# Two mixture layers of a transformer block: put-back behind the next up product, another routing sequence

## The chip, the cores and the metric

The kernel runs on one core of a Trainium2 chip. The core has TensorE (matrix products; PE in the rows), VectorE (DVE), ScalarE (ACT), GpSimd (POOL) and SyncE (SP), which here only issues DMAs, and DMA engines that bring the weights from memory. Each engine works through its own instructions in order and waits on semaphores for the others. The metric is the device time of one execution in microseconds.

## The reference

A block of two layers with mixtures of experts is followed by a second block of four layers without them. Only the mixtures are touched. Each takes 256 tokens of 1024 features, 16 experts in four groups of four, and two experts a token:

```python
scores = sigmoid(hf @ router_w)                      # 256 x 16
sel = (scores + router_bias).reshape(n, 4, 4)
group_score = top_k(sel, 2)[0].sum(-1)
g = argmax(group_score)                              # one group a token
in_group = take_along_axis(sel, g_idx, axis=1)[:, 0]
_, local = top_k(in_group, 2)                        # two experts in it
w = take_along_axis(scores, idx) ; w = w / w.sum()
combine = sum(one_hot(idx, 16) * w[..., None], axis=1)
for e in range(16):
    a = silu(hf @ w_gate[e]) * (hf @ w_up[e])        # 1024 -> 512
    y = y + combine[:, e:e+1] * (a @ w_down[e])      # 512 -> 1024
```

`hf` is the normalised and modulated input; the result, times a gate, is added to the residual stream `x`.

## The kernel before

Layer 0 of the mixtures runs from about 204 to 481 us of the profiled execution, layer 1 from about 655 to 923 us. `_moe` (L1289) does one layer.

Routing (`route`, L1172): TensorE transposes `x` into `xT` (L1181), ScalarE copies it out (L1183); 16 products give the logits with `xT` as the stationary side (L1188); VectorE scales them (`lg`), ScalarE takes the sigmoid (`sc`), and VectorE ranks experts in their groups and then the groups (`ranks`, L1214: greater, equal, three adds, a sum) down to the 0/1 choice `top` (L1234) and the weights `comb` (L1241). Meanwhile `x` times the inverse norm is kept as a rounded high part `hh` (ScalarE, L1202) and a low part `hl` (ScalarE L1206 and GpSimd L1207). Both are shown as `hTh` and `hTl` in the rows. Prefix sums of `top` on TensorE (L1303 to L1307) give each token its place `pos` (L1313) among the 64 slots of its expert.

`gather(g)` (L1327) serves four experts: a one-hot matrix `oh` (VectorE, L1335) is multiplied with high and low parts (32 products, four PSUM banks, L1344), the banks are scaled into `xgt`, masks `back` for the way home are made (L1357, L1359), and the combine weights `cs` in slot order (L1366).

Then experts follow one another. `up(e+1)` (L1396) is 16 products in two halves of eight (L1405; gate and up side by side in column tiles of 64, so two run as a pair), then ScalarE copies them out. `act(e)` (L1412) is four transposes (L1418), silu on ScalarE and a product `sg` on VectorE. `down(e)` (L1424) is eight products (L1430); behind it VectorE scales (`dg`, L1435), ScalarE takes the high part `dv` (L1436) and VectorE the low part (L1437). `put_back(e)` (L1440) adds both parts to the four accumulators with eight products (L1447).

Weights, 6 MiB an expert, come through SyncE's queue in 1 MiB transfers. `fetch` takes the places in turn from a string `HOMES`: "r" a buffer of the common ring of five, "h" a pair of half-size buffers (six pairs), "x" a buffer of a ring of its own (`WX`, two). `MF` names the experts behind which loads for the next modulation are put into the same queue.

The order on each engine isn't the order of the code: a list scheduler of the framework picks, for each engine, the next instruction from its own costs. `issue_after(i)` keeps what is written in its scope behind instruction `i` in that order.

Of the kernel before, what the change touches and what calls it, by code (L numbers as in the profile page):

```python
# [20 lines left out]
S = 256  # L21
# [9 lines left out]
GU = 2  # L31
# [3 lines left out]
WX = 2  # L35
HOMES = "rhrhxhrhrhxhr"
# [47 lines left out]
class Net:  # L84
# [636 lines left out]
    def prepare(self):  # L721
# [32 lines left out]
        nc.vector.memset(self.ones, 1.0)  # L754

# [416 lines left out]
    def route(self, outer, r, hh, hl, rwA, rb, rsh, AS):  # L1172
# [4 lines left out]
        for tok in range(NT):  # L1177
            for half in range(2):
                ps = self.pacc()
                for k in range(4):  # L1180
                    nc.tensor.transpose(ps[:, k * 128:k * 128 + 128],  # L1181
                                        x[:, tok, half * 512 + k * 128:half * 512 + k * 128 + 128], self.ident)
                nc.scalar.copy(xT[:, half * 4:half * 4 + 4, tok * 128:tok * 128 + 128],  # L1183
                               ps.rearrange("p (k t) -> p k t", k=4))
# [28 lines left out]
        def ranks(v, n, name):  # L1213

            gt, eq, rk = t(name + "g", n, 4, 4), t(name + "e", n, 4, 4), t(name + "r", n, 4)
# [3 lines left out]
            nc.vector.tensor_tensor(eq, ot, me, OP.is_equal)  # L1219
            for i in range(4):  # L1220
                if i:
                    nc.vector.tensor_tensor(gt[:, :, i, 0:i], gt[:, :, i, 0:i], eq[:, :, i, 0:i], OP.add)
# [12 lines left out]
                                       top, op0=OP.is_lt, op1=OP.mult)  # L1235
        nc.vector.tensor_tensor(ts, top, sc, OP.mult)
# [6 lines left out]
        return top, comb  # L1243

    def router(self, layer, A, SH):
# [7 lines left out]
        rwA = self.b1.tile([128, 8, 16], F32, name="rwA", tag="rwA")  # L1253
        nc.vector.tensor_tensor(rwA, rw, A[:, :, None].to_broadcast([128, 8, 16]), OP.mult)
# [34 lines left out]
    def _moe(self, layer, G, router, hh, hl):  # L1289
# [7 lines left out]
        top, comb_ = self.route(outer, r, hh, hl, *router)  # L1297
# [7 lines left out]
        nc.tensor.matmul(ps[:, 16:32], self.ones, top[:, 0, :], start=False, stop=True)  # L1305
        for tok in range(NT):
            nc.tensor.matmul(ps[0:1, 32:48], self.ones[:, 0:1], top[:, tok, :], start=tok == 0, stop=tok == 1)  # L1307
        comb = outer.tile([128, NT, 16], F32, name="combk", tag="combk", bufs=1)
# [3 lines left out]
        pos = outer.tile([128, NT, 16], F32, name="pos", tag="pos", bufs=1)  # L1312
        nc.vector.scalar_tensor_tensor(pos, ps[:, 0:32].rearrange("p (t e) -> p t e", t=NT), 1.0, top, op0=OP.add,  # L1313
                                       op1=OP.mult)
# [12 lines left out]
        def gather(g, bank=self.pat):  # L1327


            oh = self.wk.tile([128, NT, 4, CAP], F32R, name="oh", tag="oh", bufs=1)  # L1330
# [4 lines left out]
            i = nc.vector.tensor_tensor(oh, self.slot[:, None, None, :].to_broadcast([128, NT, 4, CAP]),  # L1335
                                        pos[:, :, 4 * g:4 * g + 4, None].to_broadcast([128, NT, 4, CAP]), OP.is_equal)
            yield i
            for d0 in range(0, 8, 2):
                ps = bank()
                pds = [ps[:, d * 256:d * 256 + 256] for d in range(2)]  # L1340
                for d, pd in enumerate(pds, d0):
                    for s, src in enumerate((hh, hl)):
                        for tok in range(NT):
                            mm(pd, src[:, tok, d * 128:d * 128 + 128], oh[:, tok].rearrange("p e s -> p (e s)"),  # L1344
                               start=s == 0 and tok == 0, stop=s == 1 and tok == 1)
# [50 lines left out]
        def up(e, res):  # L1396
# [4 lines left out]
            for m in range(2):  # L1401
                ws = [fetch(near(w[e], 4 * m, 4), 4, 512) for w in (wg, wu)]
                for k in range(4):
                    for j in range(2):
                        mm(ps[j * CAP:j * CAP + CAP, :], xg[:, 4 * m + k, e % 4, :], ws[j][k],  # L1405
                           start=m == 0 and k == 0, stop=m == 1 and k == 3)
# [7 lines left out]
        def act(gu):  # L1414
# [4 lines left out]
            sg = self.wk.tile([128, 4, CAP], F32, name="sg", tag="sg")  # L1419
# [4 lines left out]
        def down(e, sg):  # L1424
# [9 lines left out]
            t = self.wk.tile([128, 512], F32, name="dg", tag="dg", bufs=1)  # L1434
# [16 lines left out]
        steps = gather(0, self.pacc)  # L1451
        last = next(steps)
        with self.tc.issue_after(last.ins):
            for _ in steps:
                pass
            cur = []
            for _ in up(0, cur):
                pass
# [3 lines left out]
        for e in range(16):  # L1462
# [8 lines left out]
            if dv is not None:  # L1471
                put_back(e - 1, dv)
# [180 lines left out]
```

## Time and profile before

| | us |
|---|---|
| median of three runs | 2383.67 (2382.63 to 2385.36) |
| profiled execution | 2383.23 |
| its span in the trace | 2381.4 |
| TensorE busy | 2255.3 (95%) |
| VectorE busy | 1285.7 (54%) |
| ScalarE busy | 986.2 (41%) |
| GpSimd busy | 10.3 |

The span runs from the first to the last instruction; the 1.8 us beyond it lie around the program. Busy shares are means over stages of different kinds; the two mixture layers, some 545 us of the 2381, are read by windows of their own below. In a row of the timeline stand the start, the length, the engine and line, what is written and read, and in brackets how long the engine had been idle and for whom. Matmuls overlap their neighbours a little, so steps are measured from start to start.

### The profile page before, as it was taken

How to read it: one execution, taken by the hardware profiler on the slowest of the kernel's cores; microseconds unless marked ns; L12 is line 12 of the kernel's file. 1: busy time of each engine (PE TensorE's matmuls, PEld its weight loads, DVE VectorE, ACT ScalarE, POOL GpSimd, SP SyncE). 2: the span in 40 equal slices, each digit the busy share in tenths (PEclk: the TensorE clock that was granted, in tenths of full speed). 3: DMA queues.
4: the chain of work that ended last, by engine and by line, in shares of the span. 5: the costliest groups of instructions: out<-in, count | busy, mean ns of one | idle time of the engine just before them, and what ended most of it. 6: DMA issues, size and time to landing. Idle time of an engine off the chain costs nothing.

```text
span 2381.4 us, 34230 instructions
## 1 busy us (share of the span) xinstructions
PE 2255.3 (95%) x13802; PEld 1763.2 (74%) x13802; DVE 1285.7 (54%) x2518; ACT 986.2 (41%) x1620; POOL 10.3 (0%) x12
## 2 busy tenths in 40 slices
PE   6998999979989997999999998999999999999998
PEld 3897433268954334888899897988988898887987
DVE  4885121288632115565655666555886556666554
ACT  3544111156431113443544564444664444434443
POOL 0000000000000000000000000000000000000000
PEclk9998999979889998999999999999999999999999
DMA  8877999967679995445566534555544565454552
GB/s 309 291 264 286 404 390 409 341 213 255 243 298 415 415 408 189 166 142 176 175 212 204 190 95 136 193 168 181 174 138 159 168 204 187 145 177 142 186 169 88
DMA packets 250056, 541.99 MB, mean 228 GB/s; under 512 B 15752, under 2 KB 158720, under 8 KB 236576
## 3 DMA queue, kind: packets, MB, share of 16 engines
q1 hardware_dynamic: 239936, 531.99, 63.0%
q10 hardware_dynamic: 9952, 7.70, 1.1%
q8 instruction: 113, 1.85, 0.3%
q14 instruction: 55, 0.45, 0.1%
HBM read 538.57 MB, written 4.22 MB: 228 GB/s over the span
## 4 chain that ended last, share of the span: by engine, by line
PE 53%; DVE 5%; ACT 1%; issue 1%; DMA 1%; ACTq 0%; SPq 0%; DVEq 0%
DVE wl L157 2%; ACT wh L156 1%; DVE rsa L263 0%; DVE rsy L267 0%; PE acc__mlp__13096 L201 0%; PE acc__mlp__19954 L201 0%; PE acc__mlp__9809 L201 0%; PE acc__mlp__13097 L201 0%; PE acc__mlp__16544 L202 0%; PE acc__mlp__19955 L201 0%; PE acc__mlp__16544 L201 0%; PE acc__mlp__9810 L203 0%; PE acc__mlp__13096 L202 0%; PE acc__mlp__19955 L203 0%; PE acc__mlp__9810 L201 0%
## 5 line engine op out<-in xcount | busy, mean ns | idle before, releaser
L157 DVE TENSOR_TENSOR wl<-raw,wh 128x1024 fp32r<-128x1024 f32 (+4 forms) x526 | 614.7, 1188 | 379.4 <-ACT wh L156 375.8
L156 ACT CAST wh<-raw 128x1024 fp32r<-128x1024 f32 (+4 forms) x526 | 524.6, 1023 | 477.0 <-issue 60.2
L833 DVE SCALAR_TENSOR_TENSOR macc<-raw,c,macc 128x1024 f32<-128x1024 f32 x84 | 107.4, 1278 | 0.4
L402 ACT CAST aTh<-rl 128x512 fp32r<-128x512 f32 x56 | 34.8, 621 | 78.5 <-DVE rl L400 78.5
L539 ACT ACTIVATE p<-p,m 128x128 f32<-128x128 f32 (+1 forms) x128 | 57.1, 448 | 19.7 <-DVE m L537 19.6
L1436 ACT CAST dv<-dg 128x512 fp32r<-128x512 f32 x32 | 19.8, 618 | 102.4 <-DVE dg L1435 102.4
L280 ACT ACTIVATE junk<-x 128x512 f32<-128x512 f32 x52 | 32.8, 631 | 66.5 <-DVE x L345 36.3
L403 DVE TENSOR_TENSOR aTl<-rl,aTh 128x512 fp32r<-128x512 f32 x56 | 38.8, 692 | 38.5 <-ACT aTh L402 38.5
L400 DVE TENSOR_TENSOR rl<-rl 128x512 f32<-128x512 f32 x56 | 38.4, 685 | 0.0
L263 DVE SCALAR_TENSOR_TENSOR rsa<-rsy,rsh 128x1 f32<-128x1 f32 x186 | 34.5, 217 | 2.6
L1437 DVE TENSOR_TENSOR dv<-dg,dv 128x512 fp32r<-128x512 f32 x32 | 22.1, 691 | 18.3 <-ACT dv L1436 18.3
L222 ACT CAST hTh<-xg 128x512 fp32r<-128x512 f32 (+1 forms) x36 | 21.1, 606 | 14.4 <-DVE xg L219 14.3
L1447 PEld LDWEIGHTS acc__moe__2303<-dv,back 64*128 64x128 f32 x32 | 5.7, 186 | 25.8 <-ACT dv L1436 16.3
L267 DVE SCALAR_TENSOR_TENSOR rsy<-rsa,rsy 128x2 f32<-128x2 f32 (+2 forms) x141 | 22.7, 161 | 3.2
L539 ACT ACTIVATION_READ_ACCUMULATOR p<-p,m 128x1 f32 x128 | 24.3, 190 | 0.0
L1447 PE MATMUL acc__moe__2303<-dv,back 64*128 64x512 f32 x32 | 15.2, 494 | 9.3 <-ACT dv L1436 8.3
L223 DVE TENSOR_TENSOR hTl<-xg,hTh 128x512 fp32r<-128x512 f32 (+1 forms) x36 | 23.4, 672 | 0.3
L1447 PEld LDWEIGHTS acc__moe__6191<-dv,back 64*128 64x128 f32 x32 | 5.4, 183 | 24.1 <-ACT dv L1436 14.3
L1447 PE MATMUL acc__moe__6191<-dv,back 64*128 64x512 f32 x32 | 14.3, 477 | 7.0 <-ACT dv L1436 6.5
L1447 PE MATMUL acc__moe__2304<-dv,back 64*128 64x512 f32 x32 | 15.4, 497 | 0.0
L502 DVE TENSOR_SCALAR oss<-oss 128x1 f32<-128x1 f32 x16 | 2.5, 154 | 22.2 <-ACT junk L501 22.2
L1447 PE MATMUL acc__moe__6192<-dv,back 64*128 64x512 f32 x32 | 14.3, 477 | 0.0
(3879 smaller groups left out, 7278.5 us busy)
## 6 DMA issues: line engine op xcount, KB each, us to landing
raw<-in_w_up_dram SPq DMA_DIRECT2D x64, 1024.0 KB
raw<-in_w_down_dram SPq DMA_DIRECT2D x64, 1024.0 KB
raw<-in_w_mod_dram SPq DMA_DIRECT2D x48, 1024.0 KB
raw<-in_ret_w_in_dram SPq DMA_DIRECT2D x48, 1024.0 KB
raw<-in_exp_w_gate_dram SPq DMA_DIRECT2D x40, 1024.0 KB
raw<-in_exp_w_down_dram SPq DMA_DIRECT2D x34, 1024.0 KB
raw<-in_exp_w_up_dram SPq DMA_DIRECT2D x30, 1024.0 KB
wh<-in_exp_w_up_dram SPq DMA_DIRECT2D x34, 512.0 KB
```

What stands on the lines that cost most here:

```text
L156: nc.scalar.copy(h[:, :m * n], p)
L157: eng.tensor_tensor(l[:, :m * n], p, h[:, :m * n].bitcast(F32), OP.subtract)
L223: nc.vector.tensor_tensor(lo[:, k0:k0 + n, tok * 128:tok * 128 + 128], pv, d.bitcast(F32), OP.subtract)
L263: nc.vector.scalar_tensor_tensor(a[:, c], y[:, c], h[:, c], y[:, c], op0=OP.mult, op1=OP.mult)
L267: nc.vector.scalar_tensor_tensor(y, a, 1.5, y, op0=OP.add, op1=OP.mult)
L280: self.sq = nc.scalar.activation(junk[:, :w], p, AF.Square, scale=n ** -0.5, accum_out=ss[:, i, j:j + 1]).ins
L400: nc.vector.tensor_tensor(rl, rl, rl, OP.mult)
L402: nc.scalar.copy(h, rl)
L403: nc.vector.tensor_tensor(aT[1][:, 2 * j:2 * j + 2, :].rearrange("p k t -> p (k t)"), rl, h.bitcast(F32), OP.subtract)
L539: nc.scalar.activation(p[:, m, :], p[:, m, :], AF.Exp, bias=mx[:, m:m + 1], accum_out=rs[:, m, s:s + 1])
L833: i = nc.vector.scalar_tensor_tensor(acc, r[:, k, :], self.c[:, kk:kk + 1], acc, op0=OP.mult, op1=OP.add)
L1447: mm(acc[tok][half], back[c, e % 4, tok * 128:tok * 128 + 128], dv[j][c, :], start=e == 0 and j == 0, stop=e == 15 and j == 1)
```

## The change

- `put_back(e - 1)` is issued behind the last matmul of the first half of the next up product (`half_up`).
- Buffers: the ring `x` has three places (`WX`), with a new string `HOMES` of 14 places; `gu` takes turns between two pools; `sg` uses the tiles `hm` of the modulation, `dg` two tiles of another pool; `oh` sits in the outer pool.
- Logits: `rwA`, padded to 32 columns, is now the stationary side, and four column tiles each sum two of the eight parts; a copy and two products with `four` (four identities under one another) add them up. One of the four copies of `xT` goes to VectorE.
- `ranks` has three comparisons and a sum: ties are handled by "greater or equal" in the lower triangle.
- `pos` and the first `oh` come ahead of `comb`, `most` and the others; the low parts are made by VectorE behind that `oh`, from `x`, the norm and `hh` in one operation each; GpSimd and the copies `xn` on ScalarE are gone.
- The first gather begins with the high parts of four of its eight slices; then the first up product follows before its masks and combine weights.

The core of the diff:

```diff
-WX = 2
-HOMES = "rhrhxhrhrhxhr"
+WX = 3
+HOMES = "rhxhrhrxhrhrxh"
...
+        pl = self.pat()
+        for k in range(8):
+            j = 32 * (k % 4)
+            nc.tensor.matmul(pl[j:j + 32, 0:S], rwA[:, k, :], xT[:, k, :], start=k < 4, stop=k >= 4)
+        lT = self.cm.tile([128, 512], F32, name="xg", tag="xg")[:, 0:S]
+        nc.scalar.copy(lT, pl[:, 0:S])
         pr = self.pat()
         for tok in range(NT):
-            for k in range(8):
-                nc.tensor.matmul(pr[:, tok * 16:tok * 16 + 16], xT[:, k, tok * 128:tok * 128 + 128], rwA[:, k, :],
-                                 start=k == 0, stop=k == 7)
+            nc.tensor.matmul(pr[:, tok * 16:tok * 16 + 16], lT[:, tok * 128:tok * 128 + 128], self.four, start=True,
+                             stop=True)
...
-                for half in range(2):
-                    c = slice(half * 512, half * 512 + 512)
-                    xn = self.cm.tile([128, 512], F32, name="xg", tag="xg")
-                    nc.scalar.mul(xn.rearrange("p (k q) -> p k q", k=4), xv[:, half], r[:, tok:tok + 1])
-                    nc.gpsimd.tensor_tensor(hl[:, tok, c], xn, hh[:, tok, c].bitcast(F32), OP.subtract)
...
             nc.vector.tensor_tensor(gt, ot, me, OP.is_gt)
-            nc.vector.tensor_tensor(eq, ot, me, OP.is_equal)
-            for i in range(4):
-                if i:
-                    nc.vector.tensor_tensor(gt[:, :, i, 0:i], gt[:, :, i, 0:i], eq[:, :, i, 0:i], OP.add)
+            nc.vector.tensor_tensor(gt[:, :, 2:4, 0:2], ot[:, :, 2:4, 0:2], me[:, :, 2:4, 0:2], OP.is_ge)
+
+            two = gt.rearrange("p n i j -> p n (i j)")[:, :, 4:15:10]
+            nc.vector.tensor_tensor(two, v[:, :, 0:3:2], v[:, :, 1:4:2], OP.is_ge)
...
+        first_oh, i = one_hot(0)
+        with self.tc.issue_after(i.ins):
+            for m in range(2):
+                c = slice(m * 512, m * 512 + 512)
+                for tok in range(NT):
+                    nc.vector.scalar_tensor_tensor(
+                        hl[:, tok, c].rearrange("p (k q) -> p k q", k=4), x[:, tok, c].rearrange("p (q k) -> p k q", k=4),
+                        r[:, tok:tok + 1], hh[:, tok, c].rearrange("p (k q) -> p k q", k=4).bitcast(F32), op0=OP.mult,
+                        op1=OP.subtract)
...
+            if early:
+                pss = [bank() for _ in range(4)]
+                for d in range(0, 8, 2):
+                    part(pss[d // 2][:, 0:256], d, 0)
...
                 if m == 0:
+                    self.half_up = i.ins
                     yield
-            t = self.wk.tile([128, 512], F32, name="gu", tag="gu", bufs=GU)
+            pool, tag = (self.jk, "junk") if e % 2 else (self.wk, "gu")
+            t = pool.tile([128, 512], F32, name="gu", tag=tag, bufs=1)
...
-            sg = self.wk.tile([128, 4, CAP], F32, name="sg", tag="sg")
+            sg = self.mods.tile([128, S], F32, name="hm", tag="hm", bufs=HM).rearrange("p (f c) -> p f c", c=CAP)
...
-            t = self.wk.tile([128, 512], F32, name="dg", tag="dg", bufs=1)
+            t = self.cm.tile([128, 512], F32, name="xg", tag="xg")
...
             if dv is not None:
-                put_back(e - 1, dv)
+                with self.tc.issue_after(self.half_up):
+                    put_back(e - 1, dv)
```

What this does to the order of the instructions is shown at three places. Tile names end in numbers that differ between the two programs; line numbers shift too (before and after: up L1405 and L1438, transposes L1418 and L1453, down L1430 and L1465, put-back L1447 and L1482, gather L1344 and L1365).

TensorE, layer 1, around the start of the up product of expert 13 (`pj`), with the down product of expert 12 (`at` from `sg` or `hm`). Before:

```order
L1430 MATMUL at__moe__7216<-wh,sg 64x512 x2
L1430 MATMUL at__moe__7216<-wl,sg 64x512 x2
L1418 MATMUL at__moe__7252<-ident,gu 128x128 x4
L1430 MATMUL at__moe__7216<-raw,sg 64x512 x4
L1405 MATMUL pj__moe__7237<-wh,xgt 64x512
L1447 MATMUL acc__moe__6191<-dv,back 128x512
L1447 MATMUL acc__moe__6192<-dv,back 128x512
L1447 MATMUL acc__moe__6193<-dv,back 128x512
L1447 MATMUL acc__moe__6194<-dv,back 128x512
```

Now:

```order
L1465 MATMUL at__moe__7179<-wh,hm 64x512 x2
L1453 MATMUL at__moe__7213<-ident,gu 128x128 x4
L1465 MATMUL at__moe__7179<-wl,hm 64x512 x2
L1438 MATMUL pj__moe__7200<-raw,xgt 64x512 x8
L1438 MATMUL pj__moe__7200<-wh,xgt 64x512
L1482 MATMUL acc__moe__6158<-dv,back 128x512
L1482 MATMUL acc__moe__6159<-dv,back 128x512
```

Six more rows of put-back follow here, and then the last seven of the up product. The put-back has moved from behind the first up matmul to behind the ninth.

TensorE, layer 0, from the logits to the start of the gather. Before:

```order
L1188 MATMUL at__moe__2107<-rwA,xT 128x16 x16
L1303 MATMUL at__moe__2177<-top,first 128x16
L1304 MATMUL at__moe__2177<-top,first 128x16
L1305 MATMUL at__moe__2177<-top,ones 128x16
L1307 MATMUL at__moe__2177<-top,ones 1x16 x2
L1319 MATMUL at__moe__2191<-ident,pos 16x128 x2
L1344 MATMUL acc__moe__2202<-oh,hTh 128x256 x2
L1344 MATMUL acc__moe__2202<-oh,hTl 128x256 x2
```

Now:

```order
L1192 MATMUL at__moe__2113<-xT,rwA 32x256 x8
L1197 MATMUL at__moe__2124<-four,xg 128x16 x2
L1310 MATMUL at__moe__2156<-top,first 128x16
L1311 MATMUL at__moe__2156<-top,first 128x16
L1312 MATMUL at__moe__2156<-top,ones 128x16
L1333 MATMUL at__moe__2156<-top,ones 1x16 x2
L1343 MATMUL at__moe__2182<-ident,pos 16x128 x2
L1365 MATMUL acc__moe__2191<-oh,hTh 128x256 x2
L1365 MATMUL acc__moe__2192<-oh,hTh 128x256 x2
L1365 MATMUL acc__moe__2193<-oh,hTh 128x256 x2
L1365 MATMUL acc__moe__2194<-oh,hTh 128x256 x2
L1365 MATMUL acc__moe__2191<-oh,hTl 128x256
```

The logits are eight products and two small ones instead of 16, and the high parts of four slices stand ahead of the first low part.

VectorE, layer 0, from `top` to the one-hot. Before:

```order
L1234 SCALAR_TENSOR_TENSOR top<-grr,top 128x32
L1236 TENSOR_TENSOR ts<-top,sc 128x32
L1238 TENSOR_REDUCE tot<-ts 128x2
L1239 RECIPROCAL tot<-tot 128x2
L1311 TENSOR_REDUCE most<-at__moe__2177 1x1
L1241 TENSOR_TENSOR comb<-ts,tot 128x32
L1313 SCALAR_TENSOR_TENSOR pos<-at__moe__2177,top 128x32
L1309 COPY combk<-comb 128x32
L1316 SCALAR_TENSOR_TENSOR over<-pos,combk 128x32
L1335 TENSOR_TENSOR oh<-first,pos 128x512
```

Now:

```order
L1238 SCALAR_TENSOR_TENSOR top<-grr,top 128x32
L1241 TENSOR_TENSOR ts<-top,sc 128x32
L1243 TENSOR_REDUCE tot<-ts 128x2
L1314 SCALAR_TENSOR_TENSOR pos<-at__moe__2156,top 128x32
L1244 RECIPROCAL tot<-tot 128x2
L1319 TENSOR_TENSOR oh<-first,pos 128x512
L1328 SCALAR_TENSOR_TENSOR hTl<-x,rsy,hTh 128x512 x4
L1246 TENSOR_TENSOR comb<-ts,tot 128x32
L1338 TENSOR_REDUCE most<-at__moe__2156 1x1
L1336 COPY combk<-comb 128x32
L1345 CAST posT<-at__moe__2182 16x256
L1340 SCALAR_TENSOR_TENSOR over<-pos,combk 128x32
```

`pos` and `oh` have moved ahead of `comb`, `most`, `combk` and `over`, and the four low parts have come in behind `oh`.

## Rows read from the trace of the kernel before

**Rows 1.** The page: busy time of the engines, shares of the chain.

```profile
PE 2255.3 (95%) x13802; PEld 1763.2 (74%) x13802; DVE 1285.7 (54%) x2518; ACT 986.2 (41%) x1620; POOL 10.3 (0%) x12
...
PE 53%; DVE 5%; ACT 1%; issue 1%; DMA 1%; ACTq 0%; SPq 0%; DVEq 0%
```

**Rows 2.** Windows: length, busy us of PE, PEld, DVE, ACT, POOL, clock, DMA share, GB/s.

```profile
225.69:293.62 67.93, 67.93 (x399) 31.48 (x399) 13.31 (x26) 9.31 (x18) 0.00 (x0) 1.00 0.93 365
293.62:480.59 186.97, 174.82 (x834) 63.82 (x830) 40.48 (x62) 23.12 (x44) 0.00 (x0) 0.99 0.95 374
676.30:770.21 93.91, 93.91 (x526) 41.38 (x526) 18.45 (x33) 14.19 (x27) 0.00 (x0) 1.00 0.96 382
770.21:922.98 152.77, 142.96 (x690) 51.66 (x687) 26.49 (x45) 18.41 (x35) 0.00 (x0) 0.99 0.91 364
```

**Rows 3.** Waits of TensorE, 204 to 490 us (total us, times, longest).

```profile
PE acc__moe__2303 L1447 <- ACT dv L1436: 8.3, 8, 1.6
...
PE at__moe__2957 L1366 <- DVE sg L1421: 0.9, 1, 0.9
```

**Rows 4.** The same, 655 to 930 us.

```profile
PE acc__moe__6191 L1447 <- ACT dv L1436: 6.5, 7, 1.6
```

**Rows 5.** TensorE timeline, a step of layer 1, 742 to 756 us (start, length).

```profile
742.38 0.59 PE L1405 MATMUL pj__moe__6547<-raw,xgt 128*64 128x512 f32 x1
...
745.92 0.66 PE L1418 MATMUL at__moe__6562<-ident,gu 128*128 128x128 f32 x4
746.50 0.64 PE L1405 MATMUL pj__moe__6547<-raw,xgt 128*64 128x512 f32 x1
...
750.09 0.49 PE L1447 MATMUL acc__moe__6191<-dv,back 64*128 64x512 f32 x1
...
751.21 0.50 PE L1344 MATMUL at__moe__6599<-oh,hTh 128*128 128x256 f32 x2
...
752.34 1.94 PE L1430 MATMUL at__moe__6610<-raw,sg 128*64 128x512 f32 x8
...
755.83 0.59 PE L1405 MATMUL pj__moe__6631<-raw,xgt 128*64 128x512 f32 x1
```

**Rows 6.** TensorE timeline, a late step, 868 to 885 us.

```profile
868.18 1.02 PE L1405 MATMUL pj__moe__7237<-wh,xgt 128*64 128x512 f32 x2
...
884.11 0.50 PE L1447 MATMUL acc__moe__6191<-dv,back 64*128 64x512 f32 x1 [1.56 <-ACT dv L1436]
...
884.77 1.07 PE L1405 MATMUL pj__moe__7305<-raw,xgt 128*64 128x512 f32 x2
```

**Rows 7.** Timeline of all engines, 882.5 to 884.2 us.

```profile
882.60 0.75 DVE L1435 SCALAR_TENSOR_TENSOR dg<-at__moe__7284,cs,gate 128x512 f32<-128x512 f32 x1 [0.18 <-PE at__moe__7284 L1430]
883.44 0.62 ACT L1436 CAST dv<-dg 128x512 fp32r<-128x512 f32 x1 [1.48 <-DVE dg L1435]
884.09 0.69 DVE L1437 TENSOR_TENSOR dv<-dg,dv 128x512 fp32r<-128x512 f32 x1 [0.74 <-ACT dv L1436]
```

**Rows 8.** Timeline, routing of layer 0, 206 to 219 us.

```profile
206.62 4.16 PE L1188 MATMUL at__moe__2107<-rwA,xT 128*128 128x16 f32 x32
...
210.82 0.38 DVE L1191 SCALAR_TENSOR_TENSOR lg<-at__moe__2107,rsy,rsh 128x16 f32<-128x16 f32 x2 [1.74 <-PE at__moe__2107 L1188]
...
214.29 0.19 DVE L1234 SCALAR_TENSOR_TENSOR top<-grr,top 128x32 f32<-128x32 f32 x1
...
218.39 0.77 PE L1344 MATMUL acc__moe__2202<-oh,hTh 128*128 128x256 f32 x2 [0.44 <-DVE oh L1335]
```

**Rows 9.** Timeline of TensorE at the start, 14 to 17 us.

```profile
14.32 1.94 PE L821 MATMUL at__start__161<-raw,c 128*32 128x512 f32 x8 [2.90 <-DMA raw<-in_w_mod_dram]
```

**Rows 10.** Groups of lines, 204 to 226 us.

```profile
L1206 ACT ACTIVATE xg<-x,rsy 128x512 f32<-128x512 f32 x4 | 4.6, 1204 | 0.0
```

**Rows 11.** Windows of transfers, columns as in rows 2.

```profile
230.00:462.00 232.00, 223.32 (x1121) 88.05 (x1119) 43.30 (x73) 30.09 (x57) 0.00 (x0) 0.99 0.98 388
683.00:893.00 210.00, 203.45 (x1043) 80.76 (x1041) 37.03 (x64) 28.67 (x54) 0.00 (x0) 0.99 1.01 409
```

More of the change, by code (lines that the diff above doesn't have):

```diff
@@ L754, in prepare @@
         nc.vector.memset(self.ones, 1.0)
+        self.four = self.b1.tile([128, 16], F32, name="four", tag="four")
+        nc.vector.tensor_copy(self.four, self.ident[:, 0:16])
+        for j in range(1, 4):
+            nc.vector.tensor_tensor(self.four, self.four, self.ident[:, 32 * j:32 * j + 16], OP.add)
         self.pick = self.b1.tile([128, 2], F32, name="pick", tag="pick")
@@ L1235, in route @@
                                        top, op0=OP.is_lt, op1=OP.mult)
+        yield top
         nc.vector.tensor_tensor(ts, top, sc, OP.mult)
@@ L1242, in route @@
                                 tot[:, :, None].to_broadcast([128, NT, 16]), OP.mult)
-        return top, comb
+        yield comb
     def router(self, layer, A, SH):
@@ L1252, in router @@
         nc.scalar.dma_start(rb, bass.AP(tensor=v.tensor, offset=v.offset, ap=[[0, 128], [1, 16]]))
[L1253 to L1254 removed]
+        rwA = self.b1.tile([128, 8, 32], F32, name="rwA", tag="rwA")
+        nc.vector.memset(rwA[:, :, 16:32], 0.0)
+        nc.vector.tensor_tensor(rwA[:, :, 0:16], rw, A[:, :, None].to_broadcast([128, 8, 16]), OP.mult)
         rsh = self.b1.tile([128, 16], F32, name="rsh", tag="rsh")
@@ L1296, in _moe @@
         wg, wu, wd = I["exp_w_gate"][layer], I["exp_w_up"][layer], I["exp_w_down"][layer]
-        top, comb_ = self.route(outer, r, hh, hl, *router)
+        routing = self.route(outer, r, hh, hl, *router)
+        top = next(routing)
         gA, gSH = router[3][:, 0], router[3][:, 1]
@@ L1325, in _moe, with gather @@
         mm = nc.tensor.matmul
-        def gather(g, bank=self.pat):
-            oh = self.wk.tile([128, NT, 4, CAP], F32R, name="oh", tag="oh", bufs=1)
+        def gather(g, bank=self.pat, oh=None):
             xg = self.wk.tile([128, 8, 4, CAP], F32, name="xgt", tag="xgt")
@@ L1334, in gather, with part @@
             sent.append((xg, back, cs))
-            i = nc.vector.tensor_tensor(oh, self.slot[:, None, None, :].to_broadcast([128, NT, 4, CAP]),
-                                        pos[:, :, 4 * g:4 * g + 4, None].to_broadcast([128, NT, 4, CAP]), OP.is_equal)
-            yield i
+            early = oh is not None
+            if not early:
+                oh, _ = one_hot(g)
+                yield
+            def part(pd, d, s):
+                for tok in range(NT):
+                    mm(pd, (hh, hl)[s][:, tok, d * 128:d * 128 + 128], oh[:, tok].rearrange("p e s -> p (e s)"),
+                       start=s == 0 and tok == 0, stop=s == 1 and tok == 1)
+            if early:
+                pss = [bank() for _ in range(4)]
+                for d in range(0, 8, 2):
+                    part(pss[d // 2][:, 0:256], d, 0)
             for d0 in range(0, 8, 2):
-                ps = bank()
+                ps = pss[d0 // 2] if early else bank()
                 pds = [ps[:, d * 256:d * 256 + 256] for d in range(2)]
                 for d, pd in enumerate(pds, d0):
[L1342 to L1345, printed above, removed]
+                    if not early or d % 2:
+                        part(pd, d, 0)
+                    part(pd, d, 1)
                 for d, pd in enumerate(pds, d0):
@@ L1450, in _moe @@
         sent = []
[L1451 to L1458, printed above, removed]
+        steps = gather(0, self.pacc, first_oh)
+        for _ in range(4):
+            next(steps)
+        cur = []
+        for _ in up(0, cur):
+            pass
+        for _ in steps:
+            pass
         acc = self.new_acc()
```

21 lines of the change are left out of this document (13 added, 8 removed).

## The prediction

> **What bounds the kernel now.** I read the page's head first: TensorE is busy 95% of the span and carries 53% of the chain that ended last [rows 1], so what shortens TensorE's own sequence shortens the program, and what only frees another engine does not. Then the windows of the two mixture layers, cut at the starts of products [rows 2]. The reader is to see two halves. From the first up product to expert 4 or 7 TensorE has no idle time at all (67.93 of 67.93 us, 93.91 of 93.91 us). Behind that it stands 12.15 us of 186.97 in layer 0 and 9.81 us of 152.77 in layer 1. Third, its waits there [rows 3, 4]: the put-back waits for ScalarE's high part of `dv`, 8.3 us and 6.5 us; a gather or combine product waits 0.9 us for `sg`, three times a layer. No wait of TensorE is for a weight.
>
> The timeline says why. A regular step (expert 5 of layer 1, 742.38 to 755.83 us, 13.45 us) is half an up product 3.54, transposes 0.58, the other half 3.59, put-back 1.12, a gather bank 1.13, down 3.49 [rows 5]. In a late step the put-back stands one up matmul behind the down product that it needs [rows 6]: the chain dg 0.75, high part 0.62, low part 0.69 on VectorE and ScalarE takes about 2.2 us [rows 7], the put-back at 884.11 has waited 1.56 of it, then goes in pieces among single up matmuls. Up products run in pairs of column tiles at 0.43 us a pair; one alone takes as long as a pair. That step, from 868.18 to 884.77, takes 16.59 us, where whole groups without a bank take 13.45 - 1.13 = 12.3.
>
> **Body of the layers.** The changed order has the put-back in one piece behind the first half of the next up product in nearly every step (half up, eight put-back matmuls, half up, down). The chain of 2.2 us then lies under 3.5 us of up product. To price an order I charge each unbroken group on TensorE from [rows 5]: up and down 0.43 us a pair, rounded up, plus 0.1 for the start; put-back 0.215 a pair plus 0.2; bank 1.13; transposes 0.58; the combine group 1.0; the mask group 0.11 each plus 0.1. Check on the stretches without idle time: 68.1 and 94.0 against 67.93 and 93.91 [rows 2].
>
> Layer 1 behind 770.21: the old order costs 137.5 by these rates; the trace's 152.8 is that, 9.8 idle and 5.5 of stretched groups (put-backs whose second pair waits for the low part). The new order costs 133.4; four times in nine steps a single matmul still stands alone beside a gather or combine piece. Waits that remain: 1.6 at the last expert, where no up product is left to lie over the chain, and about 2.3 at gather or combine pieces that still follow the transposes directly. Stretching stays in fewer broken steps: 0.9. Together 138.2, a gain of 14.6. Layer 0 behind 293.62: the old order costs 167.5, and 12.2 idle and 7.3 stretched make 187.0; the new one 163.8, plus waits of 6.4 (its last two experts keep put-back pieces directly behind their down products) and 1.3: 171.5, a gain of 15.5. Bounds: with every group whole, layer 1 would be 9 ups, 10 downs, 11 put-backs, 10 transposes, 5 banks, masks and combines = 126.0, so at most 26 can go; at least the put-back's named waits without the tails go, 4.9 + 5.2. VectorE and ScalarE are busy under a quarter of the time there [rows 2]; `sg`, `dg` and `gu` now share buffers with tiles whose other users stand at the layer's start or behind its end, which I cost at nothing: if one of them did hold a buffer, its step would wait for an operation of VectorE, 0.7 us.
>
> **Routing, per layer.** Before, 32 rows of logit matmuls run 206.62 to 210.78, and `lg` follows at 210.82 [rows 8]. Now eight matmuls of 256 columns go in four column tiles. The nearest row is the start's product, the same form with 512 columns: eight records, 1.06 us each, in 1.94 us [rows 9]; half the columns twice is again about 1.9, of which the first round lies beside the last copies of `xT` (one moved to VectorE). Behind them come a copy, about 0.5, and two small matmuls. `lg` comes at about 209.9: -0.9 (bounds 0 and -1.5). Ranking drops one comparison and two small adds in each of two ranks at 0.1 to 0.2 each: -0.55. From `top` (214.29) to the first gather (218.39) go 4.1 us, in which `pos` and the one-hot `oh` stand behind `most`, `comb` and others on VectorE; now they follow the prefix sums directly: some 1.4 for these, 0.9 for the two, and latencies, 2.85 in all: -1.25. The mask matmuls (0.55) move from ahead of the first up product to behind it, where they cost the same and are counted in the 68.0 and 94.3 that the new order's early stretches give: -0.5.
>
> The gather itself takes 6.8 us, with one wait for GpSimd's low parts in it. Now eight high-part matmuls go first, and VectorE makes the four low parts behind `oh`. No row has this operation. A contiguous one of that size is 0.75 [rows 7]; but it reads `x` in steps of four, and ScalarE's read of the same view takes 1.20 for 512 columns, against 0.62 for 512 contiguous [rows 7, 10]. At 0.75 the gather gains 0.85 and never waits; at 1.45 (double) the second low part comes 0.9 late, the `xgt` scalings behind it on VectorE about 1, and the gather loses up to 0.6. I take -0.4. The Trainium skill (SBUF — State Buffer, Specifications) says that fp32 read a 16-byte line at a time falls short of full bandwidth, which speaks for the slow end; ScalarE's rows agree, and by it alone the two layers together would lose some 2 us of what I count. Sum of routing: -0.9 - 0.55 - 1.25 - 0.5 - 0.4 = -3.6 a layer, -7.2 in all, bounds -2.2 and -4.2 a layer. TensorE's clock in the gather I leave as it was.
>
> **Rest.** The new constant `four` costs four small operations at the start, +0.5 at most (0 if the loads hide it). Behind the layers the next phase needs weights and a norm; its loads come 15 us earlier where TensorE comes 18 earlier, so I charge 2.0 in all (1 to 3).
>
> **Transfers.** Each layer draws 96 MiB in order on one queue, at 388 GB/s in 230 to 462 and 409 in 683 to 893 [rows 11]; the last expert's weights land at about 462 and 893, where transfers stop being busy throughout [rows 11], some 19 and 30 us before TensorE ends. One more `wx` buffer holds 14 MiB ahead, and the first buffer comes free about 4 us earlier. So some 82 MiB (86 MB) from 676 at 409 GB/s land at 886, and in layer 0, with four MiB of modulation weights among them (90 MB), from 227 at about 447; TensorE then needs 7 us behind the last landing, and by the sum above ends 905 and 462. Transfers become the second bound, 8 to 12 us off.
>
> **Sum.** -14.6 - 15.5 - 7.2 + 0.5 + 2.0 = -34.8 against the profiled execution's 2383.2 (span 2381.4 and 1.8 around it): 2348.4. That execution lies 0.4 below the median of 2383.67, so 2349.
>
> **Rivals.**
> First, only what the trace names goes: waits of 4.9 and 5.2 on `dv` and the routing, while broken pairs cost elsewhere what they cost here. For it: the new order still has broken steps, and the old order's 12.8 us of stretched time (5.5 and 7.3) are my remainder, not rows. Against it: the check on two stretches, to 0.2 us. It gives -10.1 - 7.2 + 2.5 = -14.8, 2369. Chance 0.08.
> Second, transfers bind. At layer 0's 388 GB/s rather than 409, layer 0 ends at 227 + 233 + 7 = 467 and layer 1 at 676 + 222 + 7 = 905, 5 and 0 later than by my sum; some 3 more where waits on both sides don't overlap: 2357. For it: transfers were busy 1.01 of 683 to 893 with TensorE not waiting; the layers have never been asked for more. Against: 409 was reached in that very stretch. Chance 0.18.
> Third, slower. The new cycle of homes puts three transfers in `wx` per turn on one in-order queue; if its head stands behind a buffer that a late reader holds (a modulation load waits for `macc` on VectorE), the rate falls. The point from which it decides is about 362 GB/s, where the two layers together end as late as before; at 358 layer 0 (90 MB from 227, and 7 us) ends at 486 and layer 1 (86 MB from 676) at 923, 5.4 and 0.2 later than in [rows 2], and with the start's 0.5 that is 2390. Nothing in the order of that queue repeats such a stall every expert. Chance 0.03.
> A fourth, more gain than forecast: broken steps cost little and whole ones 12.3; half of the way to the bound of 126.0 in layer 1, and as much in layer 0, is some 11 more, about 2338. Chance 0.08.
>
> **How the numbers follow.** The forecast as summed has 0.63; its own range, from routing's bounds, stretched steps and carry, is 2341 to 2357. The range, with transfers binding and most of the first rival's way, is 2337 to 2366; outside lie that rival's far end, the slow case and very large gains, under 0.2. A measurement of this kernel can tell 0.2%, about 4.8 us, from no change. Faster by more: 0.94; within: 0.03 (a slow transfer case that just cancels the gain); slower: 0.03.
>
> **What would show it.** Right: late put-backs without a wait but for the last expert, steps of about 12.3 us where no gather stands, the first up product at about 222 and 673 us, TensorE never waiting for a load. The step on the low parts is read from VectorE's four operations (0.75 or 1.4). Wrong: waits for DMA in front of up or down matmuls behind 350 or 800 us; put-backs again waiting for `dv`; half clock reaching into the first up product.

## The result, and the profile after

The changed kernel takes 2354.0 us (median of 4 runs, 2352.8 to 2356.6), the kernel before 2384.3 (4 runs, 2382.6 to 2385.4): ratio 0.9875, 95% interval 0.9863 to 0.9888, 30.3 us less. Forecast were 34.8 less, 2349, with a range of 2337 to 2366. A second set of runs, beside the experiments, gave 2355.6 and 0.9883 (0.9867 to 0.9899).

The page first: busy time by engine, then the chain by engine (the answers to [rows 1]). The span is 2354.5 us in this execution.

```profile
PE 2239.9 (95%) x13778; PEld 1758.0 (75%) x13778; DVE 1293.3 (55%) x2526; ACT 976.4 (41%) x1612; POOL 0.2 (0%) x4
...
PE 54%; DVE 5%; ACT 1%; issue 1%; DMA 1%; ACTq 0%; SPq 0%; DVEq 0%
```

TensorE's busy time fell by 15.4 us, the span by 26.9; what else went is waiting. GpSimd is gone from the layers. The next rows are windows of the changed kernel cut at the same products as [rows 2]: up products of expert 0 and 5 in layer 0, 0 and 7 in layer 1, ends at the last put-back. (The prediction, and the expectation of e1 below, call the cut of layer 0 "expert 4"; by the order of the rows it is expert 5's up product.) The columns are length, busy us of PE, PEld, DVE, ACT and POOL, clock, DMA share and GB/s:

```profile
223.56:296.14 72.58, 72.58 (x403) 32.73 (x403) 14.04 (x27) 9.73 (x18) 0.00 (x0) 0.93 0.92 360
296.14:469.11 172.97, 165.93 (x834) 62.78 (x831) 39.85 (x61) 23.28 (x44) 0.00 (x0) 1.00 0.99 395
660.10:754.40 94.30, 94.30 (x533) 40.81 (x532) 19.43 (x35) 14.62 (x27) 0.00 (x0) 1.00 0.96 384
754.40:893.02 138.62, 135.15 (x687) 50.83 (x686) 26.23 (x45) 18.65 (x35) 0.00 (x0) 1.00 0.97 391
```

The late stretches are 172.97 and 138.62 us long (186.97 and 152.77 before); the early one of layer 1 is about as long as before, 94.30 (93.91); the early one of layer 0 is 4.65 longer, 72.58, and its clock is 0.93. Transfers now are busy 0.99 and 0.97 of the late stretches. The clock of the late stretches is 1.00 throughout now. In the kernel before it was not: [rows 2] have 0.99 there, and behind that mean stands, in that execution, a piece at half clock in each layer, behind a group of combine weights:

```profile
342.70:346.10 3.40, 3.40 (x9) 1.01 (x6) 0.91 (x3) 0.00 (x0) 0.00 (x0) 0.50 1.02 418
786.50:789.80 3.30, 3.30 (x9) 0.77 (x5) 1.04 (x2) 0.00 (x0) 0.00 (x0) 0.50 1.03 420
```

With the last put-backs of layer 0 (0.51 from 479.20 on) that is some 4 us of the 28 that the late stretches lost, an estimate: half of the busy time at 0.50. TensorE's waits there, answering to [rows 3, 4] (layer 0, then layer 1):

```profile
PE acc__moe__2292 L1482 <- ACT dv L1471: 3.1, 2, 1.6
PE at__moe__2857 L1365 <- DVE hm L1456: 0.9, 1, 0.9
```

```profile
PE acc__moe__6158 L1482 <- ACT dv L1471: 1.5, 1, 1.5
PE at__moe__6907 L1365 <- DVE hm L1456: 0.9, 1, 0.9
```

Of the waits for `dv`, 15 in all, three are left, at the ends of the layers. A late step on TensorE (expert 14 of layer 1, one behind the step of [rows 6], which is expert 13's):

```profile
859.24 0.59 PE L1438 MATMUL pj__moe__7266<-raw,xgt 128*64 128x512 f32 x1
...
862.77 0.50 PE L1482 MATMUL acc__moe__6158<-dv,back 64*128 64x512 f32 x1
...
863.89 0.64 PE L1438 MATMUL pj__moe__7266<-raw,xgt 128*64 128x512 f32 x1
...
867.38 1.89 PE L1465 MATMUL at__moe__7313<-raw,hm 128*64 128x512 f32 x8
...
870.05 0.66 PE L1453 MATMUL at__moe__7349<-ident,gu 128*128 128x128 f32 x4
...
871.55 0.59 PE L1438 MATMUL pj__moe__7334<-raw,xgt 128*64 128x512 f32 x1
```

Half up, put-back at 862.77 without a wait, half up, down with the transposes inside: 12.31 us from up product to up product. Before, this step ran from 884.77 [rows 6] to the row that follows, 15.72 us; expert 13's step went from 16.59 to 13.17.

```profile
900.49 1.07 PE L1405 MATMUL pj__moe__7373<-raw,xgt 128*64 128x512 f32 x2
```

The reader is also to see what the put-back no longer has: a bracket, that is, idle time in front of it.

Why the early stretch of layer 0 grew is seen in the clock (columns as above) and in what TensorE did there:

```profile
226.00:232.00 6.00, 6.00 (x28) 1.91 (x25) 0.99 (x2) 0.59 (x1) 0.00 (x0) 1.00 0.72 244
232.00:236.00 4.00, 4.00 (x54) 3.00 (x52) 1.22 (x4) 0.00 (x0) 0.00 (x0) 0.98 0.97 364
236.00:240.00 4.00, 4.00 (x19) 2.38 (x19) 0.47 (x3) 0.00 (x0) 0.00 (x0) 0.50 0.90 367
240.00:244.00 4.00, 4.00 (x10) 1.15 (x8) 0.00 (x0) 0.59 (x1) 0.00 (x0) 0.50 0.24 37
246.00:250.00 4.00, 4.00 (x21) 1.53 (x18) 0.33 (x1) 0.49 (x1) 0.00 (x0) 0.99 0.94 342
```

```profile
230.58 0.39 PE L1390 MATMUL at__moe__2266<-posT,identb 16*128 16x256 bf16 x2
...
232.02 1.10 PE L1399 MATMUL at__moe__2274<-combk,oh 128*64 128x1 f32 x32
...
233.97 1.95 PE L851 MATMUL at__moe__2296<-ones,macc 128*128 128x1 f32 x16
235.77 0.31 PE L883 MATMUL at__moe__2307<-ident,mod 128*8 128x128 f32 x1
...
237.92 2.88 PE L891 MATMUL at__moe__2312<-xg,ident 8*64 8x128 f32 x16
...
241.64 1.06 PE L1438 MATMUL pj__moe__2322<-raw,xgt 128*64 128x512 f32 x1
```

TensorE is busy throughout, and still its granted clock goes from 1.00 to 0.50, its lower level of 1.2 GHz, from 235.9 to 246.0 us. Ahead of the fall stand, with few up matmuls among them, the masks (L1390), 32 rows of one column (L1399), 16 of one column (L851) and a transpose. The 16 rows with eight partitions (L891) come behind it and take 2.88 us at the lower clock. Layer 1 has the same run without the modulation sums (L851), and its clock stays at 1.00 (the third window above). There L891 takes 1.57 us:

```profile
671.72 1.57 PE L891 MATMUL at__moe__6167<-xg,ident 8*64 8x128 f32 x16
```

Before the change the single columns of the combine weights stood inside the first up product and the clock stayed at 1.00 [rows 2].

Routing, layer 0 (answering to [rows 8]):

```profile
211.55 0.37 DVE L1200 SCALAR_TENSOR_TENSOR lg<-at__moe__2124,rsy,rsh 128x16 f32<-128x16 f32 x2 [0.46 <-PE at__moe__2124 L1197]
...
214.59 0.19 DVE L1238 SCALAR_TENSOR_TENSOR top<-grr,top 128x32 f32<-128x32 f32 x1
...
217.24 4.34 DVE L1328 SCALAR_TENSOR_TENSOR hTl<-x,rsy,hTh 128x512 fp32r<-128x512 f32 x4
...
217.47 0.77 PE L1365 MATMUL acc__moe__2191<-oh,hTh 128*128 128x256 f32 x2
...
223.56 0.64 PE L1438 MATMUL pj__moe__2235<-raw,xgt 128*64 128x512 f32 x1
```

Counted from the layer's first transposes (204.30 before, 206.32 here) the first up product starts after 17.24 us instead of 21.39; in layer 1 after 17.5 instead of 21.3.

### The profile page after: what moved, and what is told of

Same layout as the page of the kernel before. It is cut to its first block, busy times and chain, and to the rows that moved or that the text cites. A ratio compares the mean times of both kernels' runs of the same rounds, so it can differ in the third digit from the quotient of the medians.

```text
span 2354.5 us, 34130 instructions
## 1 busy us (share of the span) xinstructions
PE 2239.9 (95%) x13778; PEld 1758.0 (75%) x13778; DVE 1293.3 (55%) x2526; ACT 976.4 (41%) x1612; POOL 0.2 (0%) x4
## 4 chain that ended last, share of the span: by engine, by line
PE 54%; DVE 5%; ACT 1%; issue 1%; DMA 1%; ACTq 0%; SPq 0%; DVEq 0%
DVE wl L156 2%; ACT wh L155 1%; DVE rsa L262 0%; DVE rsy L266 0%; PE acc__mlp__16505 L200 0%; PE acc__mlp__9771 L202 0%; PE acc__mlp__19915 L200 0%; PE acc__mlp__13057 L201 0%; PE acc__mlp__9770 L200 0%; PE acc__mlp__9769 L202 0%; PE acc__mlp__19917 L201 0%; PE acc__mlp__19915 L201 0%; PE acc__mlp__16506 L200 0%; PE acc__mlp__16505 L201 0%; PE acc__mlp__13057 L200 0%
## 5 line engine op out<-in xcount | busy, mean ns | idle before, releaser
L1471 ACT CAST dv<-xg 128x512 fp32r<-128x512 f32 x32 | 19.8, 618 | 96.0 <-DVE xg L1470 96.0
L1472 DVE TENSOR_TENSOR dv<-xg,dv 128x512 fp32r<-128x512 f32 x32 | 22.1, 691 | 19.1 <-ACT dv L1471 19.1
L1482 PEld LDWEIGHTS acc__moe__2292<-dv,back 64*128 64x128 f32 x32 | 4.9, 184 | 18.6 <-issue 12.2
L1482 PEld LDWEIGHTS acc__moe__6158<-dv,back 64*128 64x128 f32 x32 | 4.9, 184 | 14.8 <-issue 10.5
L1482 PE MATMUL acc__moe__2292<-dv,back 64*128 64x512 f32 x32 | 12.5, 456 | 3.5 <-ACT dv L1471 3.1
L649 DVE TENSOR_REDUCE qss<-sq 128x8 f32<-128x512 f32 x16 | 10.9, 683 | 5.4 <-ACT sq L648 5.2
L1482 PE MATMUL acc__moe__6158<-dv,back 64*128 64x512 f32 x32 | 12.2, 452 | 1.7 <-ACT dv L1471 1.5
L851 PE MATMUL at__latpre__4130<-ones,macc 128*128 128x1 f32 x16 | 3.5, 351 | 9.8 <-DVEq L1289 9.8
```

Source lines behind the costliest of these rows:

```text
L1482: mm(acc[tok][half], back[c, e % 4, tok * 128:tok * 128 + 128], dv[j][c, :], start=e == 0 and j == 0, stop=e == 15 and j == 1)
```

## The experiments

Times are medians with the ratio to the kernel before in the same set of runs. "A layer" is the time from its first transposes to its last put-back in the trace: 276.3 and 268.0 us before, 262.8 and 250.4 in the changed kernel.

**The changed kernel again (e1).** No edit.

> The changed kernel once more. In its first trace the early stretch of layer 0, from the first up product to that of expert 4, took 72.6 us where 68.0 were forecast, with TensorE's granted clock at 0.50 from about 236 to 245 us. Theory A (the new order itself puts masks, combine weights, modulation sums and gate halves into one run, and the clock falls there): the stretch is 72 to 73 us again, half clock at the same place, time 2352 to 2357. Theory B (it was that execution): the stretch is 68.0 at full clock and the profiled time is near 2350.

2355.6 us, 0.9883 (0.9867 to 0.9899). The layers are 262.8 and 250.0. The step of expert 1 in layer 0 took 22.8 us in both executions, with half clock at the same place: theory A. (It was 14.9 before, but the combine weights then stood one step earlier, in the first up product, and the masks ahead of it; the two first steps together went from 25.75 to 30.4.)

**Without the hold (e2).**

```diff
-                with self.tc.issue_after(self.half_up):
-                    put_back(e - 1, dv)
+                put_back(e - 1, dv)
```

> The changed kernel without the hold on the put-back alone (the scope of issue_after around it removed); routing and buffers as changed. Theory A (the body's gain of 14 us a layer is the put-back's place): 28 us back, about 2382, with put-backs waiting for dv some 7 us a layer. Rival (only the named waits of 5 us a layer hang on it, buffers and routing bring the rest): about 2364.

2377.6 us, 0.9969 (0.9960 to 0.9978): 22 us of the 29 come back, less than the 28 of the theory, more than the rival's 8. The trace is that of the slowest of ten executions (2384.1). The waits for `dv` are back in both layers:

```profile
PE acc__moe__2292 L1482 <- ACT dv L1471: 8.8, 8, 1.8
...
PE acc__moe__6158 L1482 <- ACT dv L1471: 6.4, 6, 1.6
```

The late stretch of layer 1 (from expert 7's up product) is 150.7, that of layer 0 from the same product 147.3, where before had 152.8 and 150.9 and the changed kernel 138.6 and 137.3. So 10 to 12 us a layer hang on the hold here, and some 2 to 4 go otherwise. In layer 1 the half clock of the kernel before explains most of that: it isn't there in e2, and it had cost 1.7 by the estimate above.

**The hold alone (e3).** The kernel before, with nothing but the hold (the first half's last matmul noted as `half_up`, and the `issue_after` around `put_back`).

> The kernel before with nothing changed but the hold on the put-back; old buffers, old routing, low parts on GpSimd. Theory A: all of the body's gain, 2384 - 28 = 2356, or a few us more if combine weights and gathers fall worse. Rival one (named waits only): 2374. Rival two (the third wx buffer is needed for a body that is 28 us shorter, transfers bind without it): TensorE waits for loads, 2360 to 2368.

2355.9 us, 0.9886 (0.9869 to 0.9903): all of the gain, with old buffers and old routing. The late stretches, both cut at expert 7's up product, were 150.9 and 152.8 before and are here:

```profile
327.32:465.05 137.73, 131.56 (x673) 49.12 (x672) 32.25 (x49) 16.74 (x32) 0.00 (x0) 1.00 1.02 413
756.05:893.63 137.58, 132.33 (x690) 50.58 (x687) 26.25 (x45) 18.29 (x35) 0.00 (x0) 1.00 1.00 402
```

Waits for `dv` are 3.1 and 1.5 us, as in the changed kernel. The layers are 260.1 and 254.3. In layer 0 that is less than the changed kernel's 262.8: what routing saves there (4.1 us) is lost again to the lower clock and to another order of gather pieces. In layer 1 it is 3.9 more; the first up product there starts 22.86 us after the transposes, 1.5 later than before the change in the same order, as more of its gather ran at half clock. Both rivals fall: more than the named waits went, and no third `wx` place was needed. Beside the hold, routing and buffers then brought nothing that the times can tell (intervals 0.9869 to 0.9903 here, 0.9867 to 0.9899 in e1).

**Gate halves early (e4).**

```diff
         top = next(routing)
+        gates = self.gate_halves(G)
...
         acc = self.new_acc()
-        gates = self.gate_halves(G)
```

> The changed kernel with the gate halves, and in layer 0 the modulation sums ahead of them, written right behind the routing's choice, so that on TensorE they stand between the logits and the prefix sums, where it waits 3.4 us for top. Theory A (that wait is free room, and without these products the run of small ones behind the first up product no longer halves the clock): 3.5 + 1.7 us out of the busy stretches and 4.6 of half clock, about 2344. Rival (their three small VectorE operations stand in the chain to top and the products at half clock outlast the wait): gain under 3, 2351 to 2354.

2349.7 us, 0.9853 (0.9838 to 0.9867), some 6 better than the changed kernel in the same set (e1) where 10 were expected. The half clock behind the first up product is gone (46.5 us to expert 4 in both layers, 55.1 and 48.5 before the edit). But in layer 0 the products didn't fit into the wait. On TensorE, and then on VectorE:

```profile
212.27 2.76 PE L851 MATMUL at__moe__2156<-ones,macc 128*128 128x1 f32 x16
...
215.68 2.88 PE L891 MATMUL at__moe__2172<-xg,ident 8*64 8x128 f32 x16 [0.42 <-DVE xg L885]
218.49 0.61 PE L1311 MATMUL at__moe__2182<-top,first 128*128 128x16 f32 x2
```

```profile
215.06 0.17 DVE L853 TENSOR_TENSOR mod<-at__moe__2156,vcols 128x8 f32<-128x8 f32 x1 [2.23 <-PE at__moe__2156 L851]
...
215.55 0.17 DVE L1214 TENSOR_TENSOR sel<-sc,rb 128x32 f32<-128x32 f32 x1
```

They run largely at the lower clock (L851 2.76 us, L891 2.88). More than that, the rival's other half is seen: `sel`, where the ranking begins, stands on VectorE behind the small operations of the modulation, the first of which waits 2.23 us for L851. So `top` comes 5.4 us after `lg` instead of 3.0, the prefix sums start 2.6 us later after the logits than in the changed kernel, and the first up product stands at 20.6 instead of 17.2. In layer 1, without L851, the products were free (17.0).

**Masks and combine weights first (e5).**

```diff
-        cur = []
-        for _ in up(0, cur):
-            pass
         for _ in steps:
             pass
+        cur = []
+        for _ in up(0, cur):
+            pass
```

> The changed kernel with masks and combine weights of the first gather written ahead of the first up product again, as before the change; on TensorE the masks then stand ahead of it and the combine weights inside it, some 7 us before the modulation sums and gate halves. Theory A (the clock halves in layer 0 because all these small products stand in one run): no half clock behind the first up product, the stretch to expert 4 loses the 4.6 us, time about 2350. Theory B (the modulation sums and gate halves alone do it in the changed kernel): half clock stays, 2354 to 2356.

2350.0 us, 0.9863 (0.9842 to 0.9884). On the trace theory A holds: from the first up product to that of expert 4 the clock stays at 1.00, with the same modulation sums and gate halves in place.

```profile
224.72:275.20 50.48, 50.48 (x291) 22.77 (x290) 9.55 (x20) 7.72 (x15) 0.00 (x0) 1.00 0.93 368
```

50.5 us with the combine weights in it, where the changed kernel has 55.1. The masks' 0.55 stand ahead of it again, so layer 0 gains 3.9 (258.9), and the interval of the ratio alone would not have told this from the changed kernel.

**Old homes (e6).** `WX = 2` and the old string.

> The changed kernel with the old string of homes and two places in the wx ring, 13 MiB ahead instead of 14. Theory A (TensorE is still the bound, transfers have some us to spare): 2353 to 2357, no TensorE wait for a load, and the last expert's loads issued within 2 us of the changed kernel's. Rival (transfers are the bound of the shorter body and need the third place): TensorE waits for loads in the second half, 2359 to 2365.

2354.4 us, 0.9893 (0.9878 to 0.9908); layers 262.9 and 251.8; no wait of TensorE for a load. Layer 1 is 1.4 and 1.9 longer than in the two traces of the changed kernel, and its late stretch has two pieces of some 3.4 us at half clock (from 769.0 and 830.5) that those don't have, worth some 3.4 us by the estimate above; that the third place itself brings anything isn't shown.

**The whole step chained (e7).** On top of e4, each piece of a step is held behind the one before:

```diff
+    @contextmanager
+    def behind(self):
+        bb = self.nc.cur_bb.bb.instructions
+        n = len(bb)
+        with self.tc.issue_after(self.pe_last):
+            yield
+        for i in bb[n:]:
+            if i.engine == self.pe_last.engine:
+                self.pe_last = i
...
+            with self.behind():
+                next(ups, None)
...
+            with self.behind():
+                next(steps, None)
+            if dv is not None and e < 15:
+                with self.behind():
+                    put_back(e - 1, dv)
+            with self.behind():
+                next(ups, None)
+            with self.behind():
+                next(steps, None)
+            downs = down(e, sg)
+            with self.behind():
+                next(downs)
+            if nxt:
+                with self.behind():
+                    sg = act(nxt[0])
+            was = dv
+            with self.behind():
+                dv = next(downs)
...
```

> On top of the early gate halves, TensorE's pieces in each expert's step are written in the order wanted and each is held behind the one before: half up, gather piece, put-back, half up, gather piece, half down, transposes of the next expert, half down; the last two put-backs behind the last down. No single up matmul is left. Theory A (broken groups cost what the rates say, some 13 us a layer): steps 12.3 without a gather piece, layer 1 about 11 shorter; layer 0 limited by transfers, whose last loads land 9 to 15 us before its end now, so 4 to 10 shorter; time 2330 to 2337. Rival (the rates overstate broken groups, only named waits go): 2343 to 2346. If transfers bind in both layers: waits for loads on TensorE and 2338 to 2343.

2330.2 us, 0.9777 (0.9760 to 0.9793): 24 us below the changed kernel, and 18 to 20 below e4, on which it stands. A step with masks and one with combine weights follow; no up matmul stands alone any more.

```profile
751.17 0.39 PE L1402 MATMUL at__moe__6742<-posT,identb 16*128 16x256 bf16 x2
...
752.41 1.94 PE L1479 MATMUL at__moe__6750<-raw,hm 128*64 128x512 f32 x8 [0.63 <-DVE back L1404]
754.27 0.66 PE L1465 MATMUL at__moe__6761<-ident,gu 128*128 128x128 f32 x4
...
756.63 0.59 PE L1450 MATMUL pj__moe__6779<-raw,xgt 128*64 128x512 f32 x1
...
760.06 1.10 PE L1411 MATMUL at__moe__6794<-combk,oh 128*64 128x1 f32 x32
761.09 0.50 PE L1496 MATMUL acc__moe__6147<-dv,back 64*128 64x512 f32 x1
```

Layer 1 is 239.1 us, and from the first up product to the end 221.9 instead of 232.9 (232.4 in e4), the 11 of the theory; layer 0 from the first up product takes 228.3 (237.3 in e4). There TensorE waits for weights in the up and down products of the last expert:

```profile
PE at__moe__3566 L1479 <- DMA raw<-in_exp_w_down_dram: 1.4, 1, 1.4
PE at__moe__3566 L1479 <- DMA wh<-in_exp_w_down_dram: 1.2, 1, 1.2
PE pj__moe__3496 L1450 <- DMA raw<-in_exp_w_up_dram: 0.5, 1, 0.5
```

This is the first kernel here in which TensorE waits for a weight, and only in layer 0, whose queue carries modulation weights as well.

**Low parts read in storage order (e8).**

```diff
-                        hl[:, tok, c].rearrange("p (k q) -> p k q", k=4), x[:, tok, c].rearrange("p (q k) -> p k q", k=4),
-                        r[:, tok:tok + 1], hh[:, tok, c].rearrange("p (k q) -> p k q", k=4).bitcast(F32), op0=OP.mult,
+                        hl[:, tok, c], x[:, tok, c], r[:, tok:tok + 1], hh[:, tok, c].bitcast(F32), op0=OP.mult,
```

> The changed kernel with VectorE reading x and the high part in storage order for the low parts, so each low part belongs to other columns than its high part (this part of the result is not computed); sizes and order stay. It prices the read in steps of four: in the changed kernel the operation takes 1.09 us. If the step of 16 bytes costs, 0.75 each, and with four of them 1.3 us less on VectorE; the first up product starts at most 0.3 us earlier, since the gather on TensorE does not wait for low parts. If the step is free on VectorE and 1.09 is the price of this operation itself, it stays 1.09.

One execution. The operation by its line in the changed kernel (ns: least, median, most; the 1.09 above is the distance of starts), and then here:

```profile
L1328 DVE SCALAR_TENSOR_TENSOR hTl<-x,rsy,hTh x8: 1142/1153/1165, 217.2 to 656.7; 128x512 fp32r<-128x512 f32 x8
```

```profile
L1328 DVE SCALAR_TENSOR_TENSOR hTl<-x,rsy,hTh x8: 743/744/745, 214.8 to 653.8; 128x512 fp32r<-128x512 f32 x8
```

The steps of four cost 0.41 us an operation, 1.6 a layer on VectorE. The first up product starts at 16.98 and 16.92 us instead of 17.24 and 17.5 (17.25 and 17.03 in e1): 0.3 earlier in layer 0, and in layer 1 nothing beyond the scatter of kernels with this gather (16.9 to 17.5). TensorE's gather, not VectorE, ends last.

**Chained, modulation loads last (e9).** `MF = {5: 1, 15: 3}`.

> The chained kernel with the three modulation loads that stood behind the down loads of experts 13, 14 and 15 of layer 0 all behind expert 15's, so that they no longer stand ahead of the last expert's weights in the queue. In the chained kernel layer 0 from expert 7's up product to its end took 134.8 us against 128.4 in layer 1, with waits for loads. Theory A (that difference is transfers): 129 to 130 there, and no later start of the next phase, since TensorE waits some 9.8 us for the norm behind the layer anyway: ratio to before 0.9755 or less, about 5 us below the chained kernel. Rival (the same bytes only move behind the layer, and the next phase's modulation sums wait for them): layer 0 is shorter and the next phase later by the same, no change.

2331.9 us, 0.9793 (0.9773 to 0.9813): no change against e7. Layer 0 did become 5.1 us shorter (243.8), but the next phase starts 1.7 later after it and then waits for its sums:

```profile
PE at__latpre__4130 L851 <- DVEq L1300: 11.6, 1, 11.6
PE at__latpre__4238 L851 <- DVE macc L836: 4.9, 1, 4.9
```

In e7 the first of these was 9.8 and the second 0.7: the rival. Theory A's stretch did come (129.7 from expert 7's up product), so that difference was transfers; but what it saved was lost again behind the layer.

## Why the prediction was right, and where it was short

*Bound.* TensorE was the bound and stayed it. e3 shows the put-back's place as the cause by itself (-28.7 us), e2 the other way round (+22). That buffers had to change for it was not claimed, and e6 shows that they did not have to.

*Body.* Forecast 171.5 and 138.2, measured 172.97 and 138.62. The rates for pieces carried over: without waits, forecast 165.1 and 134.3, measured busy 165.93 and 135.15. Waits were forecast as 6.4 and 3.9, the traces have 7.0 and 3.5 idle. One reading behind it was wrong: the 7.3 and 5.5 us of the old order that the prediction put down to stretched put-backs hold some 2.3 and 1.7 of half clock (estimate, see the result). The first rival (only the named waits, 2369) falls with that, and e7 confirms the rates from the other side: with every group whole another 11 us went in layer 1, whose late stretch of 128.4 lies near the prediction's bound of 126.0.

*Routing.* Forecast -3.6 a layer, measured -4.15 and -3.8. By parts in layer 0, counted from the readiness of `x` (205.92 and 207.93): `lg` -1.3 (forecast -0.9: eight column-tile products took 1.13 us, not 1.9; on that row see the last section), ranks -0.4 (-0.55), `top` to gather 2.88 us (2.85), gather and masks -1.2 (-0.9).

*Low parts on VectorE.* Bounded by 0.75 and 1.45; 1.15 measured, in the middle, and e8 shows 0.74 for the same operation in storage order. The Trainium skill's rule (SBUF — State Buffer, Specifications: two hits in a 16-byte line are needed for full bandwidth) agrees with that. It gives no size; here it was a factor of 1.55 on VectorE. The 1.94 on ScalarE [rows 7, 10] compares two different operations and isn't shown to be the read alone. On the time it hardly counted, since the gather covers it.

*Start and carry.* Forecast +0.5 and +2.0. The start is not later (the phase behind it begins at 42.1 us before and after). Behind layer 0 the next phase starts 9.84 us after the last put-back instead of 9.32, behind layer 1 7.83 instead of 7.78.

*Where it was short.* The step that failed is "the 68.0 and 94.3 that the new order's early stretches give". Layer 1 gave 94.30, layer 0 72.58. The term assumed the full clock behind the first gather; half clock was named as a sign to look for, but only in the first up product, and without a price. e1 shows it again, e5 that it goes when the combine weights stand elsewhere. With these 4.6 us the forecast of -34.8 would have been -30.2; measured -30.3. That the gap closes so well is partly luck. The late stretches gave 1.9 less than forecast, routing 0.8 more, and start and carry cost some 2 less; the sum also credits the masks' 0.5 a layer and never charges what they add to the early stretches. And what lies outside the two layers, whose order hardly changed, differs between executions by as much as the gap: 1837.1 us in the trace before, 1841.3 in that of the changed kernel, 1838.1 in e1 of the same kernel, and 1835.8 to 1844.7 over all traces.

*Transfers.* The second rival (2357, transfers bind) did not come: no wait for a load in the changed kernel or in e6. The time alone would not have said so, since 2354.0 lies nearer to its 2357 than to 2349. It was the right second bound, though; e7 reached it in layer 0.

What stays open: which of the small products lowers the clock. e4 and e5 each take another part of them out of the run, and each is enough. Layer 1 narrows it: masks, combine weights and gate halves in one run, without the modulation sums, kept 1.00. No run moves one group alone.

## What to carry to other kernels

Price an order by its groups, not by its waits: of the 28 us that left the two late stretches, 11 were idle time (12.15 + 9.81 before, 7.04 + 3.47 after) and 17 sat in busy time, where no wait names them. Some 4 of these went with the half clock (estimate); the rest fits single matmuls without their column-tile partner and put-backs drawn out, a split that no run shows by itself. A hold behind one instruction was enough for all of it, and a hold for each piece of the step gave 18 to 20 us more (e7 against e4). When products are moved, look at what they now stand beside: a gain of 4 us in layer 0's routing was given back a few us later by a lower clock.

## What was not expected of the hardware

TensorE fell to its lower clock while it was busy without a gap, 4.00 of 4.00 us in each window, behind a run with 32 and 16 products of one column; a pair of up records, 0.43 us at full clock, then took 0.9.

Eight products of 256 columns in four column tiles ran in 1.13 us as a whole, where the prediction took 1.9 from the start's row [rows 9], four products of 512 columns (two records each) in 1.94. That row's records last 1.06 us each, as the up records of 512 columns do at half clock (the row at 241.64 above) and not 0.59 as at full clock (859.24). The clock column reads 1.00 at the start, so why they are as long as that stays open; as a price for full clock the row was too long.
